# Four heads' scores in one block, one bank for compress, and a new order of issue in a one-core decoder trunk

## The chip, the cores and the metric

The kernel runs on one core of one Trainium2 chip. The metric is the device time of one execution in microseconds (us). Three runs of the kernel before gave a median of 301.23 us (300.06 to 302.16).

## The reference, cut to what matters

A decoder trunk of two layers over 256 tokens of width 1024, all in float32, batch 1. Each layer normalises x, scales and shifts it by vectors worked out from the conditioning vector c ("ada": a 1024 x 3072 product per layer), mixes, multiplies by a third ada vector (the gate) and adds to x.

```
for layer in range(2):
    shift, scale, gate = split(silu(c) @ w_ada[layer] + b_ada[layer], 3)
    h = rms_norm(x, norm_g[layer]) * (1 + scale) + shift
    y = even_mixer(h, ...) if layer == 0 else odd_mixer(h, ...)
    x = x + gate * y
return rms_norm(x, final_g)
```

Layer 0 (the even mixer) projects h to 13 pieces. Part A is a sliding-window attention of eight heads with one key head and learned sinks. Part B has eight query heads in two groups and three branches whose results are weighted by gates and added: attention over compressed keys and values, over selected blocks, and over a window. The compressed keys and values come from a small network:

```
def compress_mlp(blocks, pe, w1, w2):      # 15 blocks of 32 tokens x 64, once for keys, once for values
    u = (blocks + pe).reshape(b, g, nc, 32 * 64)
    return gelu(u @ w1) @ w2               # w1: 2048 x 256, w2: 256 x 64; gelu in its tanh form
```

Each part's result is multiplied by silu of a gate projection, and both go through the output projection. Layer 1 (the odd mixer) is a causal attention of sixteen heads, again with a gate projection and an output projection.

## The kernel before, in words

**Precision.** A projection is done as three matmuls in a rounded float32 form: the operands are split into a high part (`whi`, `hhi`, `ghi`) and a rest (`wlo`, `hlo`, `glo`), and hi x hi, hi x lo and lo x hi are summed in a bank of PSUM. ScalarE (ACT) makes the high part by a copy, VectorE (DVE) the rest by a subtraction. Attention scores, values, transposes and compress run in plain float32.

**Order of issue.** No operation is issued where it is written. `record` puts each into a list, and `issue` (its line 247 is the line of nearly every row of the profile) gives them out in the order of a table of numbers, `ORDER`, written out by hand. Each engine works its own share in that order, one after the other: TensorE (PE), DVE, ACT, GpSimd (POOL) and SyncE (SP), which issues nearly all loads. `plan.group(ids)` gives several matmuls each other's dependences, so that the table may put them only behind all of them; it does not by itself keep them side by side.

**Stages of layer 0.** First, x is loaded (SP), c and small rows of constants are loaded (ACT, POOL), x is normalised and transposed, and pieces of `w_ada` give shift and scale (`start_ada`, `start_sums`: matmuls from `qT`, `gate` and `late` tiles with `cz`, 32 columns of the array each). GpSimd makes the identity matrix `ident` in the tile `ta` (a memset and an affine_select), on which all transposes depend; it also issues five small loads: four into `rows` (b_ada, norm_g, cmp_pe_k, cmp_pe_v) and the sinks into `srow`. Then the rows of `w_in_even` come one by one (`start_row`, `start_prep`, `start_mm`), and TensorE projects them into eight banks.

Next come rope, transposes into `qbT`, `kTb`, `qaT` (tiles `qT`, `late`), and `kc2`, the transposed keys and values of compress, which shares its memory with `vz`. ACT copies them from PSUM in four copies, two partitions' halves for each of two token tiles.

**Attention of four heads** (`attn_four`, called six times: `a_quad` twice, `b_pair` four times). For n = 0 and 1 it takes two banks, computes four scores (two heads or partition halves i, token tiles t with 128 and 256 keys; 64 rows of the array each), and DVE adds the mask, finds the extreme (`mn`) and writes the tile `sm`, ACT takes the exponential and its sum (`den`), DVE the reciprocal, DVE or ACT scale, TensorE transposes (`ps_pt`) and ACT copies out. `attn_values` then multiplies with the values into bank `ps_o`, and `gated` on DVE multiplies by the gate path.

**Gate paths** (`gate_path`, four in layer 0, 256 columns each): 48 projection matmuls into a bank `ps_pj`, a tanh of it on ACT into `oT`, and one operation on DVE, `oT <- (oT + 1) * ps_pj`.

**compress.** Its four weight tiles come into `raw`. For keys, then for values: DVE adds the position rows to `kc2` in two sums into a tile `t` (read with a step of eight floats), TensorE does 2 x 8 matmuls of 32 columns of the array into bank `ps_m`, ACT copies 256 columns out (`hp`), two matmuls with `sel` add up the four partial sums and transpose, and DVE and ACT apply gelu in six operations: copy (`hx`), square, scale and add, multiply (`h`), tanh on ACT (`th`), and the last product (`hg`). Keys and values each take a bank `ps_m` of their own turn.

**Banks.** There are eight: three `ps_pj`, two `ps_s`, one each of `ps_pt`, `ps_o` and `ps_m`. After the start of layer 0, the gate paths rotate over the three `ps_pj` and the scores over the two `ps_s`. From the output projection on, the rings are put together anew (`ps_po`, `ps_x1`, `ps_p1`, `ps_s1`).

Beside the attention run the ada sums of the second layer (`ada_jobs`): DVE scales and adds `w_ada` pieces of 128 x 1024 into `acc`. Then follow the output projection, layer 1, its output projection in four and five pieces, the final norm (a sum on DVE, a power on GpSimd, a scaling on ACT and DVE) and the stores.

Of the kernel before, what the change touches and what calls it, by code (L numbers as in the profile page):

```python
# [10 lines left out]
ALU = mybir.AluOpType  # L11
PSUM = bass.MemoryType.PSUM

P = 128
# [244 lines left out]
def tile_trunk(  # L259
# [65 lines left out]
    ring_warm = bank("o")  # L325
    V.memset(ones, 1.0)
    G.memset(ident, 1.0)
    G.affine_select(ident, ident, pattern=[[-1, P]], compare_op=ALU.is_equal, fill=0.0, base=0, channel_multiplier=1)
    dummy = const([P, 2], "dummy")
    A.activation(dummy[:, 0:1], ones[:, 0:1], AF.Exp)  # L330
    for _ in range(WARM):
# [1002 lines left out]
```

## Time and profile before

| what | value |
|---|---|
| median of three runs | 301.23 us (300.06 to 302.16) |
| the profiled execution | 299.65 us, span 297.6 us |
| TensorE busy | 287.4 us, 97% of the span |
| VectorE busy | 254.2 us, 85% |
| ScalarE busy | 187.7 us, 63% |
| GpSimd busy | 11.3 us, 4% |
| first projection matmul | 15.83 us |
| last projection matmul starts | 290.56 us |

Times in the rows are microseconds from the start of the span. In a row of the timeline stand start, length, engine, line, operation, what is written and read, the part of the array used (rows x columns), the shape and how many records; a bracket names an idle time before it and what ended it. A plain float32 matmul shows as two records, a transpose or a rounded one as one. Matmuls overlap, so how long one holds TensorE is read from the distance to the next start. In a row of a group stand the count, total busy time, mean length in ns, and the idle time before. Buffer numbers are left out of names, so `ps_s` stands for each of the score banks.

### The profile page before, as it was taken

Reading aid. Unit: us, or ns where it says so; the run is one execution under the profiler, and the core shown is the slowest. Engines: PE = TensorE matmul, PEld = TensorE weight load, DVE = VectorE, ACT = ScalarE, POOL = GpSimd, SP = SyncE. Lnnn points to the kernel's source line nnn. Section 1 sums busy time; section 2 is a strip of 40 time slices with the busy share of each in tenths; the row PEclk is TensorE's granted clock in tenths of the full one; section 3 lists DMA queues with packets and bytes.
Section 4 is the critical chain, followed back from the end, with each engine's and each line's share of the span. In section 5 each row is a group of like instructions: output and inputs, shape, how many; then the busy total and the mean of one; then the engine's idle time right before and its main releaser. Section 6 shows DMA issues by size and latency. Waiting matters only on the chain.

```text
span 297.6 us, 6147 instructions
## 1 busy us (share of the span) xinstructions
PE 287.4 (97%) x2280; PEld 245.8 (83%) x2280; DVE 254.2 (85%) x637; ACT 187.7 (63%) x479; POOL 11.3 (4%) x37
## 2 busy tenths in 40 slices
PE   8899999999999999999999999999999999999990
PEld 8688888896798886776777799999799989887890
DVE  1397899999999999999798659689959999997783
ACT  5356247985768989996447855365358746783611
POOL 6000000001000000000021000000000000000011
PEclk9999999999999999999999999999999999999998
DMA  7999999998999625939878682984467915305003
GB/s 238 386 388 372 388 395 361 325 284 259 365 390 343 198 91 198 384 136 337 298 239 259 213 299 94 364 259 143 141 201 240 358 53 157 127 2 211 1 2 141
DMA packets 48045, 71.73 MB, mean 241 GB/s; under 512 B 2504, under 2 KB 33552, under 8 KB 48016
## 3 DMA queue, kind: packets, MB, share of 16 engines
q1 hardware_dynamic: 47552, 70.90, 69.5%
q10 hardware_dynamic: 304, 0.40, 0.4%
q8 instruction: 18, 0.29, 0.4%
q14 instruction: 11, 0.09, 0.1%
q0 software_dynamic: 160, 0.05, 0.1%
HBM read 70.29 MB, written 1.05 MB: 240 GB/s over the span
## 4 chain that ended last, share of the span: by engine, by line
PE 81%; DVE 7%; DMA 5%; ACT 3%; SPq 1%; issue 1%; POOLq 0%; POOL 0%; DVEq 0%; ACTq 0%
PE ps_pj L247 49%; PE ps_s L247 12%; PE ps_o L247 8%; PE ps_pt L247 7%; PE ps_m L247 5%; DMA raw<-in_w_out_even_dram 2%; DMA qT<-in_w_ada_dram 2%; DVE wlo L247 2%; SPq L247 1%; ACT whi L247 1%; DVE acc L247 1%; DVE late L247 1%; DVE t L247 1%; DVE xs L247 1%; ACT late L247 1%
## 5 line engine op out<-in xcount | busy, mean ns | idle before, releaser
L247 ACT CAST whi<-raw 128x512 fp32r<-128x512 f32 (+2 forms) x116 | 71.8, 655 | 14.0 <-PE ps_pj L247 7.6
L247 DVE TENSOR_TENSOR wlo<-raw,whi 128x512 fp32r<-128x512 f32 (+2 forms) x100 | 71.5, 739 | 7.0 <-ACT whi L247 6.9
L247 PE MATMUL ps_pj<-hhi,whi 128*128 128x256 f32 x256 | 68.1, 284 | 0.0
L247 PE MATMUL ps_pj<-hhi,wlo 128*128 128x256 f32 x256 | 67.1, 284 | 0.0
L247 PE MATMUL ps_pj<-hlo,whi 128*128 128x256 f32 x256 | 66.9, 281 | 0.0
L247 PEld LDWEIGHTS ps_pj<-hhi,whi 128*128 128x128 f32 x256 | 46.8, 189 | 0.9 <-DVE oT L247 0.3
L247 PEld LDWEIGHTS ps_pj<-hlo,whi 128*128 128x128 f32 x256 | 46.5, 188 | 0.3
L247 PEld LDWEIGHTS ps_pj<-hhi,wlo 128*128 128x128 f32 x256 | 46.2, 188 | 0.3
L247 DVE SCALAR_TENSOR_TENSOR acc<-raw,cz,acc 128x1024 f32<-128x1024 f32 x24 | 30.7, 1278 | 0.1
L247 ACT ACTIVATE late<-late,mn 128x256 f32<-128x256 f32 (+1 forms) x58 | 26.0, 450 | 7.2 <-DVE mn L247 7.0
L247 PE MATMUL ps_pj<-wlo,hhi 128*128 128x512 f32 (+2 forms) x72 | 25.9, 376 | 0.0
L247 DVE SCALAR_TENSOR_TENSOR wlo<-raw,whi 128x512 fp32r<-128x512 f32 x32 | 21.0, 684 | 5.4 <-ACT whi L247 5.2
L247 PE MATMUL ps_pj<-whi,hlo 128*128 128x512 f32 (+2 forms) x72 | 25.5, 369 | 0.0
L247 PE MATMUL ps_pj<-whi,hhi 128*128 128x512 f32 (+2 forms) x72 | 24.9, 368 | 0.0
L247 PE MATMUL ps_pj<-whi,ghi 128*128 128x512 f32 (+1 forms) x56 | 20.9, 373 | 0.0
L247 ACT COPY late<-ps_pt 128x384 f32<-128x384 f32 (+1 forms) x33 | 15.9, 481 | 7.8 <-PE ps_pt L247 7.7
L247 PE MATMUL ps_pj<-wlo,ghi 128*128 128x512 f32 (+1 forms) x56 | 20.1, 366 | 0.0
L247 PE MATMUL ps_pj<-whi,glo 128*128 128x512 f32 (+1 forms) x56 | 20.1, 367 | 0.0
L247 PE MATMUL ps_pt<-ta,late 128*128 128x128 f32 x87 | 15.7, 281 | 0.3 <-ACT pcT L247 0.3
L247 PEld LDWEIGHTS ps_pj<-wlo,hhi 128*128 128x128 f32 x72 | 13.3, 188 | 2.5 <-DVE wlo L247 0.6
L247 ACT ACTIVATE t<-xs 128x512 f32<-128x512 f32 (+2 forms) x7 | 5.1, 723 | 16.1 <-DVE xs L247 14.1
L247 PEld LDWEIGHTS ps_pj<-whi,hlo 128*128 128x128 f32 x72 | 13.5, 188 | 1.5
(233 smaller groups left out, 592.5 us busy)
## 6 DMA issues: line engine op xcount, KB each, us to landing
raw<-in_w_in_odd_dram SPq DMA_DIRECT2D x16, 1024.0 KB, 5.9
raw<-in_w_ada_dram SPq DMA_DIRECT2D x8, 1024.0 KB, 5.5
raw<-in_w_ada_dram SPq DMA_DIRECT2D x16, 512.0 KB, 5.4
raw<-in_w_in_even_dram SPq DMA_DIRECT2D x8, 652.0 KB, 7.1
raw<-in_w_in_even_dram SPq DMA_DIRECT2D x5, 1024.0 KB, 10.2
late<-in_w_ada_dram SPq DMA_DIRECT2D x16, 256.0 KB, 6.3
raw<-in_w_out_even_dram SPq DMA_DIRECT2D x4, 1024.0 KB, 6.8
raw<-in_w_out_odd_dram SPq DMA_DIRECT2D x4, 1024.0 KB, 5.2
```

The source lines that it names most:

```text
L247: self.ops.append(dict(key=eng.key, deps=deps, fn=lambda: getattr(real, name)(*args, **kw)))
```

## The change

Five things change, and the table of numbers is new.

1. `attn_four` takes four banks and computes the eight scores of both n in one group; the rest follows for each n as before.
2. While layer 0's attention runs, the ring of scores has four banks (`ps_s` and two of `ps_pj`), and the gate paths have one `ps_pj`. The last output projection gets its three `ps_pj` back.
3. `compress` puts keys and values into one bank (columns 0 to 255 and 256 to 511), copies it out once, does four matmuls with `sel` into one bank, and gelu over 128 columns in four operations: square on ACT, a product on DVE, tanh on ACT, a product on DVE.
4. `kc2` is stored so that the sums of compress read it without a step; ACT's four copies out of PSUM now read with a step of sixteen floats and write blocks of eight in a row.
5. GpSimd's loads are written behind the making of `ident`, and the sinks' load goes with them.

```diff
     mn = sb([P, 2, 2, 2], "mn", 3)
...
+        pS = [[bank("s") for _ in range(2)] for _ in range(2)]
+        ids = []
         for n in range(2):
-            pS = [bank("s") for _ in range(2)]
-            ids = []
             for t, (a, b) in enumerate(((0, P), (P, 3 * P))):
                 for i in range(2):
-                    ids.append(T.matmul(pS[i][:, a:b], *qk[i](n, t), start=True, stop=True))
-            plan.group(ids)
+                    ids.append(T.matmul(pS[n][i][:, a:b], *qk[i](n, t), start=True, stop=True))
+        plan.group(ids)
+        for n in range(2):
...
-        A.copy(kc2[0:64, :, 64 * t : 64 * t + 64], ptv[0:64, :, :, 0])
-        A.copy(kc2[64:128, :, 64 * t : 64 * t + 64], ptv[64:128, :, :, 1])
+        kv8 = kc2.rearrange("p a (e b) -> p a e b", e=8)
+        for e_ in range(2):
+            es_ = slice(64 * e_, 64 * e_ + 64)
+            A.copy(kv8[es_, :, :, 8 * t : 8 * t + 8], ptv[es_, :, :, e_].rearrange("p n (b e) -> p n e b", e=8))
...
+        pm = bank("m")
...
-                src = kc2[:, 2 * n_ : 2 * n_ + 2, 8 * hf : 8 * hf + 120].rearrange("p g (b e) -> p e g b", e=8)
...
-                    src,
+                    kv8[:, 2 * n_ : 2 * n_ + 2, :, hf : hf + 15].rearrange("p g e b -> p e g b"),
...
-            pm = bank("m")
...
-                        pm[32 * q : 32 * q + 32, :256],
+                        pm[32 * q : 32 * q + 32, 256 * n_ : 256 * n_ + 256],
...
-            hp = sb([P, 256], "hp", 2)
-            A.copy(hp, pm[:, :256])
-            ph = bank("m")
-            for j in range(2):
-                T.matmul(ph[:, 32 * j : 32 * j + 32], hp[:, j * P : (j + 1) * P], sel, start=True, stop=True)
-            hx = sb([P, 64], "hx", 2)
-            V.tensor_copy(hx, ph[:, :64])
-            h2 = sb([P, 64], "h2", 2)
-            V.tensor_tensor(h2, hx, hx, ALU.mult)
-            V.tensor_scalar(h2, h2, 0.044715, 1.0, op0=ALU.mult, op1=ALU.add)
-            V.tensor_tensor(h2, h2, hx, ALU.mult)
-            th = sb([P, 64], "th", 2)
-            A.activation(th, h2, AF.Tanh, scale=0.7978845608028654)
-            hgt = sb([P, 64], "hg", 2)
-            V.scalar_tensor_tensor(hgt, th, 1.0, hx, op0=ALU.add, op1=ALU.mult)
-            hg[nme] = hgt
+        hp = sb([P, 512], "hp", 1)
+        A.copy(hp, pm)
+        ph = bank("m")
+        for j in range(4):
+            T.matmul(ph[:, 32 * j : 32 * j + 32], hp[:, j * P : (j + 1) * P], sel, start=True, stop=True)
+        ph = ph[:, :P]
+        h2 = sb([P, P], "h2", 1)
+        A.activation(h2, ph, AF.Square, scale=0.044715**0.5)
+        V.scalar_tensor_tensor(h2, h2, 1.0, ph, op0=ALU.add, op1=ALU.mult)
+        A.activation(h2, h2, AF.Tanh, scale=0.7978845608028654)
+        hk = sb([P, P], "hg", 1)
+        V.scalar_tensor_tensor(hk, h2, 1.0, ph, op0=ALU.add, op1=ALU.mult)
+        hg = {"k": hk[:, 0:64], "v": hk[:, 64:128]}
...
-    ring["ps_pj"] = [pj_banks[0:3], 0]
+    ring["ps_pj"] = [pj_banks[0:1], 0]
...
-    ring["ps_s"] = [s_banks + pj_banks[3:3], 0]
+    ring["ps_s"] = [s_banks + pj_banks[1:3], 0]
```

The first place is TensorE at the first quad of layer 0 and at compress (`late` times `qT` are scores, `raw` times `t` is compress, `whi` and `wlo` are a gate path). Before:

```order
L247 MATMUL ps_pj_94<-hlo,whi_113 128x256
L247 MATMUL ps_s_92<-late,qT_99 128x128
L247 MATMUL ps_s_93<-late,qT_99 128x128
L247 MATMUL ps_s_92<-late,qT_99 128x256
L247 MATMUL ps_s_93<-late,qT_99 128x256
L247 MATMUL ps_m_107<-raw_102,t_89 32x256 x8
L247 MATMUL ps_m_107<-raw_103,t_89 32x256 x8
```

Now:

```order
L247 MATMUL ps_pt_85<-ta,t_91 128x128 x2
L247 MATMUL ps_s_92<-late,qT_99 128x128
L247 MATMUL ps_s_93<-late,qT_99 128x128
L247 MATMUL ps_s_92<-late,qT_99 128x256
L247 MATMUL ps_s_93<-late,qT_99 128x256
L247 MATMUL ps_pj_95<-late,qT_99 128x128
L247 MATMUL ps_pj_96<-late,qT_99 128x128
L247 MATMUL ps_pj_95<-late,qT_99 128x256
L247 MATMUL ps_pj_96<-late,qT_99 128x256
L247 MATMUL ps_m_107<-raw_102,t_89 32x256 x8
L247 MATMUL ps_m_107<-raw_103,t_89 32x256 x8
L247 MATMUL ps_m_107<-raw_104,t_90 32x256 x8
```

Before, four more scores in the same two banks followed the first half of compress, and its second half came after a dozen other matmuls; now the eight scores stand side by side in four banks, and both halves of compress follow.

The second place is TensorE between the first two gate paths (`ps_pj`) of layer 0. Before:

```order
L247 MATMUL ps_pj_94<-hhi,wlo_117 128x256
L247 MATMUL ps_pj_95<-hlo,whi_110 128x256
L247 MATMUL ps_m_107<-w2v,hr 128x64 x2
L247 MATMUL ps_s_92<-late,qT_98 128x128
L247 MATMUL ps_s_93<-late,qT_98 128x128
L247 MATMUL ps_s_92<-late,qT_98 128x256
L247 MATMUL ps_s_93<-late,qT_98 128x256
L247 MATMUL ps_pt_85<-ta,late 128x128 x3
L247 MATMUL ps_pj_95<-hhi,wlo_114 128x256
L247 MATMUL ps_pj_96<-hhi,whi_112 128x256
```

Now:

```order
L247 MATMUL ps_pj_94<-hhi,wlo_117 128x256
L247 MATMUL ps_m_107<-w2v,hr 128x64
L247 MATMUL ps_s_92<-late,qT_98 128x128
L247 MATMUL ps_s_93<-late,qT_98 128x128
L247 MATMUL ps_s_92<-late,qT_98 128x256
L247 MATMUL ps_s_93<-late,qT_98 128x256
L247 MATMUL ps_pj_95<-late,qT_98 128x128
L247 MATMUL ps_pj_96<-late,qT_98 128x128
L247 MATMUL ps_pj_95<-late,qT_98 128x256
L247 MATMUL ps_pj_96<-late,qT_98 128x256
L247 MATMUL ps_pt_85<-ta,late 128x128 x2
L247 MATMUL ps_pj_94<-hhi,whi_110 128x256
```

Before, matmuls of several gate paths alternated in three banks; now a path's last matmul and the next path's first go to the same bank, with one value matmul of compress, eight scores and two transposes between. Of the six quads, four have their eight scores side by side, and two have them apart again in two fours.

The third place is GpSimd's list at the start (`ta` holds `ident`, `expo` the exponent of the roots `r`, `blk`, `parts` and `cz` are small constants). Before:

```order
L247 DMA srow<-in_a_sinks_dram 1x8x1
L247 MEMSET blk 128x6
L247 MEMSET ta 128x128
L247 MEMSET parts 128x16
L247 DMA rows<-in_b_ada_dram 48x128
L247 MEMSET blk 64x1
L247 DMA rows<-in_cmp_pe_v_dram 16x128
L247 DMA rows<-in_norm_g_dram 16x128
```

Now:

```order
L247 DMA rows<-in_cmp_pe_k_dram 16x128
L247 DMA rows<-in_cmp_pe_v_dram 16x128
L247 DMA rows<-in_b_ada_dram 48x128
L247 DMA rows<-in_norm_g_dram 16x128
L247 MEMSET parts 128x16
L247 MEMSET blk 64x1
L247 DMA srow<-in_a_sinks_dram 1x8x1
L247 MEMSET ta 128x128
L247 ISA
L247 AFFINE_SELECT ta<-ta 128x128
L247 CAST ones_r<-ones 128x128
L247 TENSOR_TENSOR r_87<-r_87,expo 128x1 x2
```

The four loads into `rows` now stand first and the sinks' load last; the making of `ident` still follows all five, and the cast of `ones_r`, which stood far behind, now stands ahead of the roots. On ACT the tanh of c moves ahead of the two squares of x.

More of the change, by code (lines that the diff above doesn't have):

```diff
@@ L319, in tile_trunk @@
         Y.dma_start(xs[:, t, :], x[0, t * P : (t + 1) * P, :])
-    G.dma_start(rows[16:64, :], b_ada.rearrange("l (k p) -> (l k) p", p=P))
-    G.dma_start(rows[0:16, :], norm_g.rearrange("l (k p) -> (l k) p", p=P))
-    G.dma_start(rows[64:80, :], cmp_pe_k.rearrange("o (i t) d -> (o i) (t d)", t=2))
-    G.dma_start(rows[80:96, :], cmp_pe_v.rearrange("o (i t) d -> (o i) (t d)", t=2))
+    snk = const([P, 16], "snk")
+    srow = const([1, 8], "srow")
     ones = const([P, P], "ones")
@@ L328, in tile_trunk @@
     G.affine_select(ident, ident, pattern=[[-1, P]], compare_op=ALU.is_equal, fill=0.0, base=0, channel_multiplier=1)
+    G.dma_start(rows[16:64, :], b_ada.rearrange("l (k p) -> (l k) p", p=P))
+    G.dma_start(rows[0:16, :], norm_g.rearrange("l (k p) -> (l k) p", p=P))
+    G.dma_start(rows[64:80, :], cmp_pe_k.rearrange("o (i t) d -> (o i) (t d)", t=2))
+    G.dma_start(rows[80:96, :], cmp_pe_v.rearrange("o (i t) d -> (o i) (t d)", t=2))
+    G.dma_start(srow, a_sinks)
     dummy = const([P, 2], "dummy")
@@ L362, in small_rows @@
             V.tensor_scalar(bs, bs, 1.0, None, op0=ALU.add)
-    snk = const([P, 16], "snk")
-    srow = const([1, 8], "srow")
-    G.dma_start(srow, a_sinks)
     def small_sinks():
@@ L595, in attn_four @@
                         out=sm[:, a:b],
-                        in0=pS[i][:, a:b],
+                        in0=pS[n][i][:, a:b],
                         in1=msk[:, 2 * P - (b - a) : 2 * P],
@@ L863, in compress @@
             w2[nme] = w2t
-        hg = {}
+        pm = bank("m")
+        kv8 = kc2.rearrange("p a (e b) -> p a e b", e=8)
         for n_, nme in enumerate(("k", "v")):
@@ L881, in compress @@
                     T.matmul(
-                        pm[32 * q : 32 * q + 32, :256],
+                        pm[32 * q : 32 * q + 32, 256 * n_ : 256 * n_ + 256],
                         uT[:, 8 * u + 4 * i + q, :, :].rearrange("p g b -> p (g b)"),
                         w1[nme][u][:, 4 * i + q, :],
-                        start=u + i == 0,
-                        stop=u + i == 2,
+                        start=n_ + u + i == 0,
+                        stop=n_ + u + i == 3,
+                        skip_group_check=True,
                         tile_position=(0, 32 * q),
@@ L1244, in tile_trunk @@
     ws = []
+    ring["ps_pj"] = [pj_banks[0:3], 0]
     spl[0] = SPL[3]
```

240 rows, old and new, of the table ORDER are left out of this document.

## The prediction

> **What bounds the kernel now.** I read the page's busy line first, then the table of stretches, then the waits of TensorE alone between 16 and 291 us.
>
> ```profile
> span 297.6 us, 6147 instructions
> PE 287.4 (97%) x2280; PEld 245.8 (83%) x2280; DVE 254.2 (85%) x637; ACT 187.7 (63%) x479; POOL 11.3 (4%) x37
> ...
> 16.00:68.60 52.60, 52.56 (x383) 46.36 (x383) 48.70 (x102) 33.57 (x78) 0.15 (x1) 1.00 1.02 351
> 68.60:84.70 16.10, 15.43 (x166) 11.21 (x164) 15.49 (x66) 10.65 (x40) 0.91 (x6) 1.00 0.97 352
> 84.70:142.00 57.30, 56.96 (x454) 44.57 (x453) 56.83 (x159) 48.64 (x140) 0.00 (x0) 1.00 0.72 253
> 142.00:160.00 18.00, 17.96 (x113) 13.42 (x113) 15.66 (x37) 9.19 (x17) 2.70 (x5) 1.00 0.76 243
> 160.00:285.00 125.00, 125.00 (x987) 112.44 (x986) 105.66 (x250) 75.95 (x186) 0.00 (x0) 1.00 0.55 181
> ...
> PE ps_s L247 <- DVE mn L247: 0.5, 1, 0.5
> PE ps_pt L247 <- ACT pcT L247: 0.3, 1, 0.3
> ```
>
> The columns of a stretch are its length and the busy time of PE, its weight loads, DVE, ACT and POOL. TensorE sets the end: from the first projection to the last it is never free for more than half a microsecond, and its two named waits in 275 us make 0.8 us. From 68.6 to 142 us, where layer 0's attention and compress lie, DVE is full as well (15.49 of 16.10, 56.83 of 57.30). After 160 us nobody makes TensorE wait. So the change pays only in three ways: TensorE's stream gets shorter, its few waits between 68.6 and 142 us go, or the ends move.
>
> **The change, part by part.** The counts of matmuls are the same in both orders, so what can shorten TensorE's stream is the price of going from one kind of matmul to another. This is TensorE at the first quad (start, length; four scores show as x8, the 32-row-wide compress matmuls of one tensor as x32):
>
> ```profile
> 68.22 0.28 PE L247 MATMUL ps_pj<-hhi,wlo 128*128 128x256 f32 x1
> 68.34 0.28 PE L247 MATMUL ps_pj<-hhi,whi 128*128 128x256 f32 x1
> 68.45 0.28 PE L247 MATMUL ps_pj<-hlo,whi 128*128 128x256 f32 x1
> 68.66 0.93 PE L247 MATMUL ps_s<-late,qT 64*128 64x128 f32 x8
> 69.52 1.93 PE L247 MATMUL ps_m<-raw,t 128*32 128x256 f32 x32
> 71.95 0.93 PE L247 MATMUL ps_s<-late,qT 64*128 64x128 f32 x8 [0.50 <-DVE mn L247]
> 72.81 0.44 PE L247 MATMUL ps_pt<-ta,t 128*128 128x128 f32 x2
> 73.00 0.36 PE L247 MATMUL ps_pj<-hhi,wlo 128*128 128x256 f32 x1
> 73.20 0.28 PE L247 MATMUL ps_pj<-hhi,whi 128*128 128x256 f32 x1
> ...
> 74.60 1.93 PE L247 MATMUL ps_m<-raw,t 128*32 128x256 f32 x32
> 76.46 0.44 PE L247 MATMUL ps_pt<-ta,t 128*128 128x128 f32 x2
> 76.66 0.36 PE L247 MATMUL ps_pj<-hhi,whi 128*128 128x256 f32 x1
> ...
> 82.50 0.27 PE L247 MATMUL ps_pt<-ta,late 128*128 128x128 f32 x1
> 82.53 0.37 PE L247 MATMUL ps_pj<-hhi,whi 128*128 128x256 f32 x1
> 82.73 0.28 PE L247 MATMUL ps_pj<-hlo,whi 128*128 128x256 f32 x1
> ```
>
> Starts of projection matmuls lie 0.12 us apart (68.22, 68.34), but the one ahead of a score block holds TensorE for 0.21 (68.45 to 68.66). A change of shape thus costs 0.09 us. What it costs on the way out is hidden in the block's 0.86 us, and I take the same 0.09 (bounds 0 and 0.09).
>
> *Scores.* Twelve blocks of four scores become four blocks of eight and four of four, since the list takes two of the six quads apart again; compress's two blocks become one. Counted over the whole TensorE order, stretches in one shape go from 64 to 56: eight changes fewer, 8 x 0.09 = **-0.7 us**. Against that, a projection matmul that follows another kind holds TensorE for 0.20 instead of 0.12 (73.00 to 73.20). Behind a transpose this costs nothing, because the last transpose is short by as much: one transpose and the projection behind it take 0.23 (82.50 to 82.73), hardly more than 0.12 and the 0.10 of a transpose in a pair (76.46 to 76.66). So the eighteen more places where transposes cut a projection are free, but places where a projection directly follows scores, values or compress matmuls go from 11 to 15: 4 x 0.08 = **+0.3 us**.
>
> *Compress.* The first 32 compress records hold TensorE from 69.52 to 71.95, 2.43 us; the second 32 begin at 74.60 and end at 76.46, 1.86 us. The difference, 0.57, is the 0.50 wait of the table: the second four scores need the banks that DVE has yet to empty. In the changed order no scores stand there, and all 64 compress records run in a row over sums that DVE makes one behind the other. I take 0.4 of the 0.57 as won, **-0.4 us** (bounds 0 and -0.6): what keys shared with values they now wait for together, and the joined chain through tanh stands before the next matmuls.
>
> ```profile
> L247 DVE COPY hx<-ps_m x2: 218/221/224, 74.3 to 77.8; 128x64 f32<-128x64 f32 x2
> L247 DVE TENSOR_SCALAR h<-h x2: 185/190/194, 76.6 to 78.3; 128x64 f32<-128x64 f32 x2
> L247 DVE TENSOR_TENSOR t<-vz,rT x4: 583/587/622, 68.0 to 73.4; 128x240 f32<-128x240 f32 x4
> L247 DVE TENSOR_TENSOR qT<-t 128x256 f32<-128x256 f32 x16 | 6.2, 415 | 0.1
> L247 ACT COPY vz<-ps_o x4: 365/368/370, 63.1 to 67.6; 64x256 f32<-64x256 f32 x4
> ```
>
> DVE loses ten operations of 64 columns (two of 0.19, eight of 0.22: 2.1 us) and gets two of 128 columns, for which there is no row: between 0.22 (64 columns) and 0.42 (256 columns), say 0.3 each. The four sums over kc2 read every eighth float at 0.59 us; read in a row they should cost what 256 columns in a row cost, 0.42 at most: 4 x 0.17 = 0.7. DVE gets about 2.1 - 0.6 + 0.7 = 2.2 us shorter, in a stretch that it fills. But TensorE there waits for little, so of 2.2 I book **-0.5 us** (bounds 0 and -1.5). ACT trades two copies and two tanh for one wider copy, a square and a tanh, about even, and has 5 us free in the stretch (10.65 of 16.10).
>
> ACT's four copies into kc2 now read PSUM with steps of sixteen floats instead of two. If each paid what the stepped sum pays, 0.17 us, it would be 0.7 us on ACT, which has that room; I book nothing. [...]
>
> *One bank for the gate paths.* From the first quad to the output projection the gate projections have one bank instead of three, so each next gate path waits until tanh and the gating operation of the last have read it.
>
> ```profile
> L247 ACT ACTIVATE oT<-ps_pj 128x512 f32<-128x512 f32 x8 | 4.8, 596 | 12.1 <-PE ps_pj L247 12.1
> L247 DVE SCALAR_TENSOR_TENSOR oT<-oT,ps_pj 128x512 f32<-128x512 f32 x8 | 5.5, 681 | 2.6 <-ACT oT L247 2.5
> L247 DVE SCALAR_TENSOR_TENSOR acc<-raw,cz,acc 128x1024 f32<-128x1024 f32 x24 | 30.7, 1278 | 0.1
> L247 DVE TENSOR_SCALAR acc<-raw,cz 128x1024 f32<-128x1024 f32 x4 | 3.0, 747 | 0.0
> L247 DVE TENSOR_TENSOR wlo<-raw,whi 128x1024 fp32r<-128x1024 f32 x16 | 19.4, 1214 | 1.1 <-ACT whi L247 1.1
> ```
>
> The reading takes 0.60 + 0.68 = 1.3 us. Between path 1 and path 2 the order puts eight scores (2 x 0.86), a value matmul and two transposes, some 2.0 us of cover, and between the next paths value matmuls too. It suffices if DVE is not behind. On DVE an ada scaling (0.75), a split (1.21) and an ada sum (1.28) stand right ahead of the gating operation. I book **+0.3 us** for the three handovers together (bounds 0 and +6, the rival below).
>
> *GpSimd's loads and the start.* The row loads go ahead of the sinks' load, ident still comes after all five, the cast of ones_r now stands ahead of the two roots, and ACT does c's tanh, which needs ident, ahead of the squares.
>
> ```profile
> 4.60 1.06 ACT L247 ACTIVATE t<-xs 128x1024 f32<-128x1024 f32 x1 [1.89 <-DMA xs<-in_x_dram]
> 5.07 0.29 POOL L247 TENSOR_SCALAR_AFFINE_SELECT ta<-ta 128x128 f32<-128x128 f32 x1
> 12.29 1.30 PE L247 MATMUL ps_m<-qT,cz 128*32 128x128 f32 x40 [0.21 <-DMA qT<-in_w_ada_dram]
> 14.59 0.62 ACT L247 CAST whi<-raw 128x512 fp32r<-128x512 f32 x1 [0.22 <-DMA raw<-in_w_in_even_dram]
> 15.18 0.60 ACT L247 ACTIVATE hhi<-bigA,shs 128x256 fp32r<-128x256 f32 x1
> 15.83 0.50 PE L247 MATMUL ps_pj<-whi,hhi 128*128 128x512 f32 x1
> 157.88 0.29 POOL L247 CAST ones_r<-ones 128x128 fp32r<-128x128 f32 x1
> ```
>
> x comes up to 0.9 us later (ACT at about 5.5 instead of 4.60; the cast's 0.29 falls into that). The w_ada pieces, which end at 12.29, cover it, and the first projection hangs on the raw load at 14.59 plus a cast and hhi on ACT, which keep their order: 15.8 again. Without the cover it would be +0.9. I book 0. The tail has the same last piece, the same root on POOL and the same two stores: 0.
>
> Sum: -0.7 + 0.3 - 0.4 - 0.5 + 0.3 = **-1.0 us**. Against the profiled execution, 299.65 us (span 297.6), that is 298.6. The runs shown have a median 1.6 us above it, 301.23, so I predict **300.2 us**, own range 298.5 to 301.9. About 1%, 3 us, is what a measurement tells from no change here.
>
> **Rivals.** *Handover waits (slower).* DVE reaches the ada scaling ahead of the gating operation only when the gate path ends. Then 0.75 + 1.21 + 1.28 + 0.68 = 3.9 us stand against 2.0 us of cover: 1.9 a handover, in which everything behind the waiting projection on TensorE stands still, as the transposes at 72.81 did behind the scores that waited at 71.95. Three times 1.9, less the 1.3 of the other terms: 301.23 + 5.7 - 1.3 = 305.6. For it: DVE is full from 84.7 to 142. Against: DVE gets 2.2 us less just there. It decides the sign once the three waits together pass 1.3 us, and tells as slower past 4.3. Chance 0.12.
>
> *DVE was the hidden bound (much faster).* If TensorE between 68.6 and 142 follows DVE through many short waits that the view gives to "issue", then DVE's 2.2 us pass on whole: -0.4 - 2.2 - 0.6 = -3.2, 298.0. For it: DVE's 56.83 of 57.30. Against: the two waits above sum to 0.8. Chance 0.15.
>
> *No effect.* Eight scores in a row save nothing because the way out of a block costs nothing (then -0.35 + 0.3), and what compress gives the one bank takes: 301.2. For it: six of twelve blocks keep four scores or are split, and TensorE's count is unchanged. Chance 0.28.
>
> **How the numbers follow.** The forecast has 0.45. Faster by over 1% (below 298.2) is the second rival and a little of the forecast's edge, 0.16; slower by over 1% (above 304.2) most of the first rival, 0.11; the rest, 0.73, is within 1%. The range must take in part of both outer cases and the unknown bounds: 297.3 to 303.2.
>
> **What would show it.** In the changed profile, eight scores should show as one block of 1.6 to 1.7 us; the compress records as one stretch of 3.7; the hx group gone and the sums over kc2 near 0.4; DVE's busy time near 252. A wait of ps_pj for DVE oT in layer 0 of more than 1 us in sum would prove the first rival; a first projection later than 16.1 us would prove the start wrong. Scores of layer 1 that come earlier by less than the end does would put the gain outside layer 0.

## The result and the profile after

| | before | after |
|---|---|---|
| median | 301.11 us (299.98 to 302.16, 7 runs) | 297.86 us (296.62 to 298.76, 7 runs) |
| the profiled execution, and its span | 299.65, 297.6 | 297.86, 296.1 |
| start of the first projection / first scores / last `pcT` x `vz` / last matmul | 15.83 / 68.66 / 140.19 / 290.56 | 15.50 / 68.88 / 137.81 / 289.05 |

`pcT` x `vz` are the last values over compressed keys; a block of other values follows in every kernel, its last start 1.4 us later. Where the text says last values, it means this point. The ratio is 0.990 (95% interval 0.987 to 0.993): 3.2 us faster, where 1.0 was forecast from a profile. The sign was right, the time lies inside the range and outside the forecast's own 298.5 to 301.9, and almost on the 298.0 of the rival that saw a hidden bound in DVE. It lies inside the range only because the range took in part of that rival. Two executions far above all others, 469.61 us of the kernel before and 719.61 of the experiment with all scores in pairs, are left out throughout.

The busy line, the stretches and TensorE's waits between 16 and 290 us, of the changed kernel:

```profile
span 296.1 us, 6150 instructions
PE 286.2 (97%) x2280; PEld 246.1 (83%) x2280; DVE 252.1 (85%) x629; ACT 187.7 (63%) x478; POOL 12.3 (4%) x37
```

```profile
68.60:84.70 16.10, 16.06 (x180) 12.42 (x179) 15.28 (x59) 13.84 (x46) 0.63 (x5) 1.00 0.95 345
84.70:142.00 57.30, 57.30 (x450) 45.59 (x451) 56.08 (x157) 48.99 (x137) 0.00 (x0) 1.00 0.75 259
```

```profile
PE ps_pj L247 <- DVE t L247: 0.7, 2, 0.5
PE ps_m L247 <- DMA late<-in_w_ada_dram: 0.3, 1, 0.3
PE ps_pj L247 <- DVE wlo L247: 0.2, 1, 0.2
```

DVE is busy for 2.1 us less, as worked out. Both waits of before (`mn`, `pcT`) are gone, and the view names none for `oT`, the handovers of the one gate bank; what the first of them costs all the same is read further down. TensorE's busy share says nothing: it is 97% in both. The first quad and compress on TensorE:

```profile
68.46 0.28 PE L247 MATMUL ps_pj<-hlo,whi 128*128 128x256 f32 x1
68.57 0.38 PE L247 MATMUL ps_pt<-ta,t 128*128 128x128 f32 x2
68.88 0.93 PE L247 MATMUL ps_s<-late,qT 64*128 64x128 f32 x8
69.64 0.82 PE L247 MATMUL ps_pj<-late,qT 64*128 64x128 f32 x8
70.39 3.66 PE L247 MATMUL ps_m<-raw,t 128*32 128x256 f32 x64
73.98 0.39 PE L247 MATMUL ps_pj<-hhi,wlo 128*128 128x256 f32 x1
74.21 0.28 PE L247 MATMUL ps_pj<-hhi,whi 128*128 128x256 f32 x1
```

Eight scores hold TensorE for 1.51 us (68.88 to 70.39); two blocks of four in the kernel before took 2 x 0.86 = 1.72. All 64 compress records are one stretch of 3.59 (70.39 to 73.98), where before there were 2.43 and 1.86. In a group's row stand count, busy time and mean in ns:

```profile
L247 ACT COPY vz<-ps_o 64x256 f32<-64x256 f32 x4 | 1.5, 367 | 0.0
L247 DVE TENSOR_TENSOR t<-vz,rT 128x240 f32<-128x240 f32 x4 | 1.5, 406 | 0.0
L247 DVE SCALAR_TENSOR_TENSOR h<-h,ps_m 128x128 f32<-128x128 f32 x1 | 0.3, 289 | 0.3 <-ACT h L247 0.3
```

Three prices came as booked: a sum over `kc2` without the step costs 0.41 (0.42 was taken), a gelu operation over 128 columns 0.29 (0.3), and the ACT copies that now read PSUM in steps of sixteen 0.37, as before. The first handover of the one gate bank:

```profile
82.57 0.60 ACT L247 ACTIVATE oT<-ps_pj 128x512 f32<-128x512 f32 x1
...
83.86 0.68 DVE L247 SCALAR_TENSOR_TENSOR oT<-oT,ps_pj 128x512 f32<-128x512 f32 x1
84.59 0.19 PEld L247 LDWEIGHTS ps_pj<-hhi,whi 128*128 128x128 f32 x1 [0.25 <-DVE oT L247]
...
84.31 0.27 PE L247 MATMUL ps_pt<-ta,late 128*128 128x128 f32 x1
84.59 0.39 PE L247 MATMUL ps_pj<-hhi,whi 128*128 128x256 f32 x1
```

DVE's last read of the bank ends at 84.54 and the next path's first matmul starts at 84.59, 0.28 us behind the start of the transpose ahead of it. At the other places of the attention where a projection follows a transpose, that distance is 0.03 to 0.09 (82.50 to 82.53 in the rows of the prediction). So this handover costs 0.25 us, and 0.27 in the second profile (85.46 to 85.76), although the transpose's row reaches to the projection and no wait is named. At the second and third handover the bank is free 0.6 us before it is needed.

**Where the time came from.** TensorE does the same 597 matmuls between the first scores and the last values of layer 0, in another order. The table gives to each kind of matmul the distance from its start to the next start, summed, in us; a wait counts with the matmul ahead of it. The lower rows are the experiments below; `warm` has the attention of before, `mixed` that of the changed kernel, and in `fours` the stretch has one projection more.

| kernel | all | scores | compress | small (sel, w2, kcbd) | projections, transposes, ada sums | values |
|---|---|---|---|---|---|---|
| before | 71.53 | 10.69 | 4.29 | 2.89 | 44.83 | 8.82 |
| before, profiled again | 71.90 | 10.77 | 4.29 | 2.88 | 45.13 | 8.82 |
| warm | 72.68 | 10.79 | 4.30 | 2.89 | 45.89 | 8.82 |
| after | 68.93 | 9.51 | 3.59 | 2.62 | 44.38 | 8.82 |
| after, profiled again | 70.14 | 9.95 | 3.59 | 2.62 | 45.17 | 8.82 |
| dose_before | 73.31 | 10.98 | 4.29 | 2.89 | 46.32 | 8.83 |
| dose_after | 70.88 | 9.88 | 3.59 | 2.62 | 45.97 | 8.82 |
| new_compress | 71.77 | 10.90 | 3.90 | 2.73 | 45.41 | 8.82 |
| old_compress | 71.52 | 10.26 | 3.73 | 2.69 | 46.03 | 8.82 |
| fours | 72.60 | 11.67 | 3.59 | 2.68 | 45.83 | 8.82 |
| all_eights | 69.99 | 9.07 | 3.59 | 2.62 | 45.88 | 8.82 |
| late_gate | 70.39 | 9.76 | 3.59 | 2.62 | 45.59 | 8.82 |
| mixed | 68.83 | 9.47 | 3.59 | 2.62 | 44.33 | 8.82 |

The first pair of profiles differs by 2.6 us here, the second by 1.8; three profiles of the old attention lie between 71.5 and 72.7, three of the new between 68.8 and 70.1. Profiles of one order differ mostly at one or two places between 111 and 117 us, where a transpose waits for ACT's `late` (two waits, 1.0 us in sum, in the second profile of the changed kernel, none in the first). Compress is 0.7 shorter in both and the small matmuls 0.27. Scores are 1.2 or 0.8 shorter; four eight-blocks in place of eight fours make 8 x 0.856 - 4 x 1.511 = 0.80 of it, and the other 0.4 of the first pair is the old wait for `pcT`; in the second pair a wait for ACT's `late` takes its place. The rest differs between the pairs: the column of projections falls by 0.45 in the one and not in the other. Outside this stretch the first pair shows -0.33 up to the first projection, +0.55 from there to the first scores, +0.55 from the last values to the first scores of layer 1 (TensorE waits for `t` and `wlo` there, 0.5 of the first row of its waits and the third) and +0.33 behind, together with the -2.6 a change of -1.5. The first scores of layer 1 come 1.8 us earlier (189.16 for 190.99) and the last matmul 1.5, so the gain is layer 0's.

### The profile page after: what moved, and what is told of

Same layout as the page of the kernel before. It is cut to its first block, busy times and chain, and to the rows that moved or that the text cites. A ratio compares the mean times of both kernels' runs of the same rounds, so it can differ in the third digit from the quotient of the medians.

```text
span 296.1 us, 6150 instructions
## 1 busy us (share of the span) xinstructions
PE 286.2 (97%) x2280; PEld 246.1 (83%) x2280; DVE 252.1 (85%) x629; ACT 187.7 (63%) x478; POOL 12.3 (4%) x37
## 4 chain that ended last, share of the span: by engine, by line
PE 54%; DVE 21%; DMA 17%; issue 3%; ACT 2%; SPq 1%; POOL 0%; POOLq 0%; ACTq 0%; DVEq 0%
PE ps_pj L247 37%; DMA raw<-in_w_in_odd_dram 8%; DVE acc L247 7%; PE ps_s L247 5%; PE ps_pt L247 4%; DVE wlo L247 4%; PE ps_o L247 4%; PE ps_m L247 4%; DMA raw<-in_w_in_even_dram 3%; DVE late L247 3%; DMA raw<-in_w_out_even_dram 2%; DVE t L247 2%; DMA qT<-in_w_ada_dram 2%; DMA late<-in_w_ada_dram 2%; ACT whi L247 1%
## 5 line engine op out<-in xcount | busy, mean ns | idle before, releaser
L247 PE MATMUL ps_pj<-hhi,whi 128*128 128x256 f32 x256 | 69.3, 286 | 0.2 <-DVE t L247 0.2
L247 PE MATMUL ps_pj<-hhi,wlo 128*128 128x256 f32 x256 | 69.3, 284 | 0.0
L247 PE MATMUL ps_pj<-hlo,whi 128*128 128x256 f32 x256 | 68.9, 284 | 0.0
L247 PEld LDWEIGHTS ps_pj<-hhi,wlo 128*128 128x128 f32 x256 | 47.0, 188 | 0.9 <-issue 0.7
L247 ACT ACTIVATE late<-late,mn 128x128 f32<-128x128 f32 (+1 forms) x58 | 26.0, 449 | 6.3 <-DVE mn L247 6.3
L247 PE MATMUL ps_pj<-wlo,hhi 128*128 128x512 f32 (+2 forms) x72 | 25.3, 376 | 0.2 <-DVE wlo L247 0.2
L247 PE MATMUL ps_pt<-ta,late 128*128 128x128 f32 x87 | 16.8, 276 | 0.0
L247 ACT ACTIVATE whi<-raw 128x512 fp32r<-128x512 f32 x16 | 9.6, 625 | 9.2 <-PE ps_pj L247 9.2
L247 PEld LDWEIGHTS ps_pj<-whi,hhi 128*128 128x128 f32 x72 | 13.3, 188 | 2.4 <-ACT hhi L247 0.4
```

The lines of the kernel that those rows point to most:

```text
L247: self.ops.append(dict(key=eng.key, deps=deps, fn=lambda: getattr(real, name)(*args, **kw)))
```

## The experiments

Two explanations stood against each other. By the first, that of my sum, TensorE's stream got shorter (fewer changes of shape, one stretch of compress) and DVE's relief counts for little. By the second, DVE had been holding TensorE in small steps, and its relief is the gain. Where an expectation sets other theories against each other, it says so. Ratios are against runs of the kernel before on the same chip.

**The changed kernel and the kernel before, once more.** No edit.

> The changed kernel once more, for its size and for a second trace. Between the two profiled executions the span fell by 1.5 us (297.6 to 296.1), between the medians of the runs the time fell by 3.2 us (301.11 to 297.86). Theory 1 (TensorE's stream and nothing else): the time falls by 1.5 to 2 us and the first medians lay apart by the chance of few runs. Theory 2 (DVE was the hidden bound, the second rival of the prediction): the time falls by about 3 us again, ratio 0.990, and the profile of before was one of its fast executions.

> The kernel before once more, for a further trace: the stretch from the first scores to the last values of layer 0 took 71.53 us in the first profile and 72.68 in the profile named warm, whose order is the same there; the changed kernel took 68.93 and 70.14. Theory 1 (a gain of 1.5 to 3 us there whatever the execution): 71.3 to 72.7. Theory 2 (the first profiles were chance): 70.5 or less.

The changed kernel: 298.11 us (6 runs) against 300.71, ratio 0.993 (0.990 to 0.995). The kernel before under a label of its own: 301.28 (12), ratio 1.000 (0.997 to 1.003). So the gain is no chance, and lies between 2.6 and 3.2 us. Some 0.3 of it is the clock at the start (last section): without the executions of before that had a mean clock of 0.990 or less, the medians on this chip are 300.38 and 298.11, 2.3 apart.

**More work on DVE**, in the kernel before and in the changed one. Fifteen operations that nobody reads are spread over DVE's queue from 72 us on, one behind every thirteenth:

```diff
+    for _ in range(15):
+        V.tensor_tensor(rows[0:96, :], tb[0:96, 0:128], tb[0:96, 128:256], ALU.add)
```

> The kernel before with fifteen added operations on DVE alone, 96x128 each (about 0.28 us by the 128-column rows, 4.2 us in all), one behind every thirteenth DVE operation of the stretch from 72 to 140 us; nobody reads what they write. Theory 1 (TensorE sets the end, DVE only keeps pace): 0 to +1 us. Theory 2 (DVE sets the end there): +4.2 us.

> The same fifteen DVE operations (4.2 us in all) in the changed kernel, compared with the changed kernel in this same set of runs. Theory 1: 0 to +0.5 us, less than in the kernel before, since DVE has 2.2 us less to do. Theory 2: DVE was the bound of before, and its 2.2 us of relief are the gain, so 4.2 us more on it cost at least 2 us here.

303.26 us (11) against 300.71, ratio 1.007 (1.004 to 1.010), and 300.02 (12), ratio 0.999 (0.997 to 1.001): +2.5 by medians (+2.2 by the ratio) and +1.9 over the changed kernel. Five of the eleven executions of the first had a mean clock of 0.990 or less, against five of 28 of before and none of the second; the medians of the others are 301.88 and 300.38, +1.5. The busy line, the operations' group and TensorE's waits of the first:

```profile
PE 290.4 (96%) x2280; PEld 247.5 (82%) x2280; DVE 256.8 (85%) x652; ACT 187.9 (62%) x479; POOL 11.3 (4%) x37
```

```profile
L254 DVE TENSOR_TENSOR rows<-tb 96x128 f32<-96x128 f32 x15 | 4.2, 282 | 0.0
```

```profile
PE ps_s L254 <- DVE mn L254: 0.5, 1, 0.5
PE ps_pt L254 <- ACT pcT L254: 0.3, 1, 0.3
PE ps_m L254 <- issue: 0.3, 1, 0.3
PE ps_pt L254 <- ACT late L254: 0.2, 1, 0.2
```

The rows sum to 4.2 us, but DVE's busy time rises by only 2.6 (254.2 to 256.8; in the changed kernel by 3.0), since the end of one operation overlaps the next (in the dosed changed kernel an added one lasts 0.28 from 73.61, and DVE's next operation starts at 73.82). So some 0.6 us of time come per microsecond of DVE in both kernels (1.5 for 2.6, 1.9 for 3.0), between what the two explanations expected. Against the two profiles of before the named waits grew by 0.5 us, the attention by 1.4 to 1.8, and 1.2 to 1.5 of that lie in the table's column of projections and transposes: set against the first profile place by place, some ten distances are longer by 0.1 to 0.3 each, and hardly a row names them. (Against `warm`, with its own wait of 0.6 for `late`, the attention grew by 0.6.) So DVE does hold TensorE there. TensorE's busy share does not show it: it is 96% both in `mixed` and in `dose_before`, whose attention takes 68.83 and 73.31 us. Where a matmul really ends no run here shows.

**DVE's relief alone**: the kernel before with parts 3 and 4 (the joined compress and the new layout of `kc2`), its own order, rings and blocks of four:

```diff
+        pm = bank("m")
...
-            pm = bank("m")
...
-                        pm[32 * q : 32 * q + 32, :256],
+                        pm[32 * q : 32 * q + 32, 256 * n_ : 256 * n_ + 256],
```

> The kernel before with parts 3 and 4 of the change alone: keys and values of compress in one bank with gelu in four operations, and the new layout of kc2. Scores stay in fours over two banks, the gate paths keep three banks, the order is that of before, with compress's later operations put where their inputs come. Theory 1: the four scores between the two halves of compress still wait for DVE (0.5 us in the profile of before), so 0 to -0.4 us. Theory 2: DVE loses its 2.2 us here as well, so -2.2 us.

301.18 us (12), ratio 1.001 (0.999 to 1.004): nothing. Its busy line, and the first 16.1 us from its first scores (70.73) on:

```profile
PE 289.1 (96%) x2280; PEld 246.7 (82%) x2280; DVE 252.3 (84%) x629; ACT 187.6 (63%) x478; POOL 11.3 (4%) x37
...
70.73:86.83 16.10, 15.79 (x165) 11.20 (x165) 13.42 (x57) 10.68 (x39) 0.90 (x6) 1.00 0.99 359
```

DVE lost its 1.9 us, and idles for them in this stretch (13.42 of 16.10; in the kernel before it is 15.49 from the first scores on). That its next work in the old order is not there yet is the likely reason. In the table compress and the small matmuls are 0.55 shorter and the other columns 0.4 to 0.8 longer than in the two profiles of before (0.4 shorter than in `warm`): what is won seems to be given back further on, one of the waits named, 0.2 us for `hg` of the joined gelu. By the runs, relief by itself pays nothing, which the second explanation in its plain form does not survive.

**The new order without the relief**: the changed kernel with compress as before, keys then values (part 3 undone):

```diff
-        hp = sb([P, 512], "hp", 1)
-        A.copy(hp, pm)
...
+            hp = sb([P, 256], "hp", 2)
+            A.copy(hp, pm[:, :256])
+            ph = bank("m")
...
+            hx = sb([P, 64], "hx", 2)
+            V.tensor_copy(hx, ph[:, :64])
```

> The changed kernel without part 3: keys and values of compress each in a turn of the bank and gelu in six operations on 64 columns twice, as before; scores, rings, kc2 and the rest of the order as changed. DVE has ten operations of 0.19 to 0.22 us more and two of 128 columns less. Theory 1 (the scores and their banks made the gain): one break more (0.4) and a wait or two, 0.4 to 1 us above the changed kernel. Theory 2 (compress and DVE's relief made it): the attention takes 71.5 us as before, 2 us above the changed kernel.

299.93 us (12), ratio 0.996 (0.993 to 0.998), 1.8 above the changed kernel's second median.

```profile
PE ps_m L253 <- DVE kcbd L253: 1.1, 1, 1.1
PE ps_pj L253 <- DVE t L253: 0.5, 1, 0.5
PE ps_pt L253 <- ACT late L253: 0.4, 1, 0.4
PE ps_m L253 <- DVE hx L253: 0.2, 1, 0.2
```

TensorE now waits 1.3 us for compress's chain on DVE (`kcbd`, `hx`). So the joined compress is worth 0.9 to 1.8 us in the new order (by the ratios and by the medians) and nothing in the old one; scores, rings and order without it give 1.3, or 0.7 against the executions of before above a clock of 0.990 (300.61). The profile shows none of it in the attention: 71.52 us, as the second explanation expected, against 71.5 to 72.7 of before. That points at the length of the chain rather than at DVE's load: ahead of the wait DVE itself idles for TensorE, 0.44 and 0.39 us at 77.66 and 78.95. One reservation: where compress's old operations go in the new list was my choice.

**One break in a block**: in each of the four blocks of eight, one projection stands between the two fours. The first of them on TensorE:

```diff
-MATMUL ps_pj_94<-hlo,whi_113 128x256
 MATMUL ps_pt_85<-ta,t_91 128x128 x2
 MATMUL ps_s_92<-late,qT_99 128x128
...
 MATMUL ps_s_93<-late,qT_99 128x256
+MATMUL ps_pj_94<-hlo,whi_113 128x256
 MATMUL ps_pj_95<-late,qT_99 128x128
```

> The changed kernel with its four blocks of eight scores taken apart into two fours each by one projection matmul put between them (five of the order's numbers move, by less than ten places on TensorE). Theory 1 (the price of a change of shape): the stretch from the first scores to the last values of layer 0, 68.93 and 70.14 us in the two profiles of the changed kernel, grows by 4 x 0.2 (two fours 2 x 0.856, a block of eight 1.511) and by 4 x 0.08 for the projections behind scores, 0.8 to 1.1 us, and the time with it. Theory 2 (DVE sets the pace there): at most 0.4 us, since TensorE would only wait less.

300.04 us (12), ratio 0.998 (0.995 to 1.000), 1.9 above the changed kernel's second median.

```profile
94.25 0.93 PE L253 MATMUL ps_s<-late,qT 64*128 64x128 f32 x8
95.11 0.39 PE L253 MATMUL ps_pj<-hhi,wlo 128*128 128x256 f32 x1
95.42 0.93 PE L253 MATMUL ps_pj<-late,qT 64*128 64x128 f32 x8
96.90 0.39 PE L253 MATMUL ps_pj<-hhi,whi 128*128 128x256 f32 x1 [0.55 <-DVE oT L253]
```

The lone projection holds TensorE for 0.31 (95.11 to 95.42) where one among its like takes 0.12, and two fours 1.72 where eight take 1.51: **a break costs 0.19 + 0.21 = 0.40 us**. Four make 1.6 of the 2.5 to 3.7 that the attention grew, more than the 0.8 to 1.1 expected. Of the rest the last row shows one part: this projection belonged to the gate path, which so ended later, and the second handover, free in the changed kernel, now costs 0.55. Another part is 1.2 us of waits for ACT's `late`, of which the changed kernel has none in one profile and 1.0 in the other.

Where the price lies, the starts inside a block tell. Two rows of the kernel before (its 68.66 and 69.52 stand in the prediction), then three of the changed kernel, where the second four of an eight follow the first:

```profile
68.88 0.50 PE L247 MATMUL ps_s<-late,qT 64*128 64x128 f32 x4
69.21 0.38 PE L247 MATMUL ps_s<-late,qT 64*128 64x256 f32 x2
...
69.43 0.38 PE L247 MATMUL ps_s<-late,qT 64*128 64x256 f32 x2
69.64 0.28 PE L247 MATMUL ps_pj<-late,qT 64*128 64x128 f32 x2
69.75 0.71 PE L247 MATMUL ps_pj<-late,qT 64*128 64x128 f32 x6
```

The last pair of a block holds TensorE for 0.31 (69.21 to 69.52), the same pair with scores behind it for 0.21 (69.43 to 69.64): the way out costs 0.10. The first pair holds it for 0.21 (68.66 to 68.88, rounded), the same pair behind other scores for 0.11 (69.64 to 69.75): the way in costs 0.10 inside the block, beside the 0.09 of the matmul ahead of it.

**All scores of layer 0 in pairs**: sixteen such breaks, counted from the changed kernel.

```diff
 MATMUL ps_s_93<-late,qT_99 128x128
+MATMUL ps_pj_94<-hhi,wlo_117 128x256
 MATMUL ps_s_92<-late,qT_99 128x256
```

> The same with all scores of layer 0 in pairs: sixteen projection matmuls between scores that stood side by side. Theory 1: 16 x 0.2 to 16 x 0.28, so 3.2 to 4.5 us longer than the changed kernel. Theory 2 (DVE sets the pace there): clearly under 2 us.

306.06 us (5), ratio 1.017 (1.014 to 1.020): 8 us above the changed kernel, 0.5 a break, where 3.2 to 4.5 in all were expected. Sixteen breaks at 0.40 make 6.4. No profile shows one of these five, so the parts of the 0.5 cannot be read.

**All scores in eights**: the two quads that the new list still takes apart are joined.

```diff
 MATMUL ps_s_93<-late,qT_98 128x256
+MATMUL ps_pj_95<-late,qT_98 128x128
+MATMUL ps_pj_96<-late,qT_98 128x128
...
-MATMUL ps_pt_85<-ta,late 128x128 x3
-MATMUL ps_pj_95<-late,qT_98 128x128
```

> The changed kernel with the two quads whose scores the order takes apart put together as well: two fours move up behind their first fours, so that all six quads have one block of eight. A projection between two fours held TensorE for 0.31 instead of 0.12 in the profile named fours, and two fours cost 0.20 more than a block of eight: 0.40 for each break. Theory 1 (the price of a change of shape): two breaks less, 0.8 us shorter between the first scores and the last values of layer 0, time 0.5 to 0.8 us below the changed kernel. Theory 2 (DVE sets the pace there): no change within 0.3 us, or longer by the wait for four free banks.

298.30 us (7), ratio 0.992 (0.989 to 0.995): no gain over the changed kernel.

```profile
PE ps_pj L253 <- DVE t L253: 0.9, 1, 0.9
PE ps_pt L253 <- ACT late L253: 0.7, 1, 0.7
PE ps_m L253 <- DMA late<-in_w_ada_dram: 0.6, 1, 0.6
PE ps_pj L253 <- DVE mn L253: 0.3, 1, 0.3
```

Scores took the 0.44 us less that two blocks should give (9.07 for 9.51), and the attention, 69.99, lies between the changed kernel's two. The wait for `mn` (0.3) stands in neither of those; the wait for ACT's `late` (0.7) has its like in the second of them (1.0), so that this order brings it on is not shown. So the 0.8 expected did not come, and only 0.3 of what took it back can be laid to this order.

**The gating operation later**: on DVE, that of three gate paths goes behind the next ada operation.

```diff
-SCALAR_TENSOR_TENSOR oT<-oT,ps_pj_94 128x512
 SCALAR_TENSOR_TENSOR acc_106<-raw_103,cz,acc_106 128x1024
+SCALAR_TENSOR_TENSOR oT<-oT,ps_pj_94 128x512
```

> The changed kernel with the gating operation of gate paths 1, 2 and 3 on DVE moved behind the ada operation that followed it (1.28, 1.28 and 0.75 us), nothing else. In the profile of the changed kernel the gating operation of path 1 ends at 84.54 and the next path begins at 84.59; of path 2 it ends at 94.23 and the next begins at 94.84. Theory 1 (the one bank leaves next to no room, as the first rival of the prediction says): waits of ps_pj for DVE oT of 1.2, 0.7 and about 0.3 us, and the time 1.5 to 2.2 us up. Theory 2 (the cover of 2.0 us suffices, as the forecast booked it): under 0.5 us.

298.57 us (9), ratio 0.993 (0.991 to 0.996).

```profile
PE ps_pj L253 <- DVE oT L253: 1.5, 2, 1.3
```

The handover wait is there at once, 1.5 us in two of three places, so the mechanism of my first rival exists. Yet the time rose by only 0.5 to 0.7 (298.57 against 298.11 and 297.86). Against the first profile of the changed kernel the attention is 1.5 us longer (70.39 for 68.93), the whole wait; against the second (70.14) 0.25, because the two waits for `late` there have gone. That a wait at the handover spares a wait further on, DVE having done in the meantime an ada operation that it had to do anyway, fits the second and the times; the first does not show it.

**The start.** In one kernel the transpose of the row loads goes behind the `w_ada` matmuls (kernel before); in another the changed kernel gets the old order ahead of the first scores, with the same move.

```diff
-MATMUL ps_pt_85<-ta,rows 128x96
 MATMUL ps_s_92<-ta,t_89 128x128
...
 MATMUL ps_o_66<-ones 128x128
+MATMUL ps_pt_85<-ta,rows 128x96
```

> The kernel before with one number of the order moved: the transpose of the small rows on TensorE, which waits for the row load of cmp_pe_k (1.0 us in the profile of before, 2.0 us in two others of the same start, after which the granted clock stands at 0.5 for 3 us), comes behind the first 64 w_ada matmuls as in the changed kernel. 5 of 28 runs of before had a mean clock of 0.990 or less and took 302.4 us, the others 300.5. Theory 1 (that wait lets the clock drop): no run with a mean clock under 0.991, first projection never later than 16.1 us, median 0.3 to 0.5 us lower. Theory 2 (the drop comes by chance): as many low clocks as before.

> The changed kernel with the order of before for everything ahead of the first scores, and the row transpose moved as in the run named warm. From the first projection to the first scores before took 52.83 us, the changed kernel 53.38 and 54.03. Theory 1 (the new order of the first stretch costs, the attention's gain is its own): that stretch takes 52.8 again, the attention 69 to 70, and the time is 0.5 to 1.2 us below the changed kernel, about 297.2. Theory 2 (what TensorE wins ahead of the attention it loses there to DVE): as the changed kernel, 298.

301.06 us (12), ratio 1.002 (0.999 to 1.005); and 298.63 (9), ratio 0.993 (0.991 to 0.996), against the changed kernel's 0.990 and 0.993. Neither gains. In the first, the idle time at the rows only moves on to the `w_ada` landing, its first projection came at 16.65 and one of its twelve executions still had a mean clock below 0.990 (304.04 us), against what the first theory expected. The second has the attention of the changed kernel (68.83), and 53.5 us from the first projection to the first scores; the changed kernel has 53.4 and 54.0, the kernel before 52.8 and 52.7. So the gain belongs to the attention. Much of the loss ahead of it is one wait for a piece of `w_ada` in the changed kernel (0.57 in its second profile), which the old order there does not have; it has one for `t` in its place, just ahead of the first scores (first row the changed kernel, second the `mixed` one):

```profile
22.97 0.53 PE L247 MATMUL ps_m<-late,cz 128*32 128x128 f32 x12 [0.35 <-DMA late<-in_w_ada_dram]
69.34 0.41 PE L253 MATMUL ps_pt<-ta,t 128*128 128x128 f32 x2 [0.52 <-DVE t L253]
```

What makes the rest (0.2 of 0.55 us in the first pair) was not found.

## Why the prediction was right, and where it was short

The direction held because the gains named for scores and compress were real. Both terms were too small, which the table shows for the stretch between 68 and 141 us. The forecast itself, 300.2, was 2.3 us off:

- *Scores*, booked -0.7 + 0.3. Measured: -0.8 for the blocks alone. The step that failed is "A change of shape thus costs 0.09 us". The 0.09 taken for the way out was right (0.10). But the 0.86 of a block hides 0.10 of the way in as well, in its first pair, and a whole break costs 0.40, where my prices make 0.09 + 0.09 + 0.08 = 0.26. The 0.3 for projections that stand behind scores, values or compress cannot be seen apart; projections, transposes and ada sums together went from 44.83 and 45.13 to 44.38 and 45.17.
- *Compress*, booked -0.4. Measured: -0.70 for its 64 records and -0.27 for the small matmuls behind them. All of the 0.57 was won, not 0.4 of it; another 0.13 (3.59 for two times 1.86) and the small matmuls in a row were not in the term.
- *DVE*, booked -0.5 of 2.2, with the reason "But TensorE there waits for little". That was read from the view of waits, and the doses show that this view does not show how DVE holds TensorE up: some 0.6 us for each microsecond of work added, more than half of it unnamed. But the rival that passed the 2.2 on whole is not shown either, and that its 298.0 was nearly hit is luck: the relief alone gave nothing. What the runs show is that the two go together. TensorE's stream gets some 1.2 us of prices and a wait of 0.57 shorter; with the old compress the new order keeps 0.7 to 1.3 of its 2.3 to 3.2, because TensorE waits for the longer chain. Whether the lighter load on DVE earns anything beside the shorter chain was not tested apart.
- *Handovers*, booked +0.3. Measured: 0.25 at the first, nothing at the other two, so the sum came as booked, though no wait names it. The other two runs of it (0.55 in one, 1.5 in the other) show how close it was.
- *Start*, booked 0. Measured: -0.33 in both pairs of profiles (15.83 to 15.50, 16.35 to 16.02), and something rarer, below.
- *Ahead of the attention* nothing was booked and 0.55 to 1.3 us were lost (52.83 and 52.68 against 53.38 and 54.03).

**What stays open** is the difference between profiles and medians. The profiled spans differ by 1.5 us, the medians by 3.2 and 2.6. I took the kernel before's 1.6 us between its profile and its median along into the forecast; the changed kernel's profile (297.86) lies on its median. From profile to profile the sum of -1.0 meets -1.8 in execution time, and -1.6 in the second pair (300.74 to 299.10). Why more executions of the kernel before lie well above its fastest is explained only in part, by the last section.

## What to carry to other kernels

Where two engines are both full, price a change on both: here relief on one paid nothing as long as the order kept the work where it was (1.9 us less on DVE, ratio 1.001), and much of a shorter stream on the other was given back as waits (1.3 us for compress's chain with the old compress). A list of waits doesn't clear an engine of holding another (2.6 us more on DVE cost 1.5 us, while the named waits grew by 0.5); adding a known dose of work to it, and reading how the time moves, shows it, and so does a distance from start to start that is longer than its like elsewhere (0.28 for 0.03 at the first handover). Here a projection put into a block of scores cost 0.40 us, so matmuls of one shape are worth keeping together; but the last two blocks of eight gained nothing (298.30 us for 298.11 and 297.86) and brought a wait of 0.3 for DVE's `mn`.

## What was not expected of the hardware

TensorE's granted clock fell at the start in some executions. Two profiles have it, of kernels with the start of before; this is the first (the transpose that waits for the row load, and the stretch behind it; the first bracket is the idle time, the third number from the end the clock):

```profile
11.54 0.27 PE L254 MATMUL ps_pt<-ta,rows 96*128 96x96 f32 x1 [1.96 <-DMA rows<-in_cmp_pe_k_dram]
...
12.65:16.06 3.41, 3.41 (x66) 2.89 (x64) 1.00 (x3) 0.60 (x2) 0.00 (x0) 0.50 1.02 390
```

TensorE waited 1.96 us for the rows, and from 12.65 on ran at a granted clock of 0.50 for 3.41 us (in the other profile, `new_compress`, 2.01 us and then 3.41 from 12.43 on); the first projection came at 18.10 instead of 15.83 to 16.35. With the idle time at 1.04 us (before) the clock stayed at 1.00, but so it did with 2.10 in the kernel whose transpose was moved:

```profile
12.13 0.42 PE L253 MATMUL ps_m<-qT,cz 128*32 128x128 f32 x8 [2.10 <-DMA qT<-in_w_ada_dram]
```

So the length of one gap does not decide it; what does was not shown. Of 92 executions of the kernel before, 16 had a mean clock of 0.990 or less and were about 1.8 us longer; so had 5 of 11 and 3 of 12 of the two experiments with its start (`dose_before`, `new_compress`), 1 of 21 with the transpose moved, and of 70 with the changed start none. That their clock, too, fell at the start is inferred from the two profiles. It makes 0.3 us of the mean difference. The clock fell not in the gap but when TensorE had been at work again for 1.11 us (11.54 to 12.65; in `new_compress` 0.93, 11.50 to 12.43).
